# A decoder layer with 32 experts: the tensor engine's order per expert written out by hand

## The chip, the cores and the metric

The kernel runs on one core of a Trainium2 chip. The metric is device time in microseconds (us): the median of the runs shown, and for the profile the time of one profiled execution. PE is the tensor engine (TensorE), PEld its weight loads, DVE the vector engine, ACT the scalar engine, POOL GpSimd, and SP the engine whose queue issues nearly all DMA transfers.

## The reference

One layer of a decoder on 256 tokens of width 1024: a token mixer, a LayerNorm, a mixture of experts, a second LayerNorm. All is float32. The change is in the experts:

```python
logits = x @ router_w + router_b                  # 256 x 32
top_v, top_i = top_k(logits, 4);  gates = softmax(top_v)
# for each expert e, on the tokens that chose it:
h = x_e @ w1[e] + b1[e]                           # 1024 -> 2048
gate, up = split(h);  gate = min(gate, 7);  up = clip(up, -7, 7)
act = (up + 1) * (gate * sigmoid(1.702 * gate))
y_e = act @ w2[e] + b2[e]                         # 1024 -> 1024
out[token] += gate_weight * y_e
x = layer_norm(ALPHA * x + out)
```

## The kernel before

The mixer and the first LayerNorm take the first 270 us or so. Then come the experts, one after the other. Every expert's weights, 8 MB for the first product and 4 MB for the second, are read once from DRAM, in transfers of 1 MB (`load_w`, L76) that SP issues in order into a ring of buffers. A transfer waits until PE has read what lay in its buffer. In the loop, iteration e loads `w1` of expert e (8 transfers) and then `w2` of expert e-1 (4 transfers).

An expert has 64 slots. `slots` (L875, DVE) compares the tokens' ranks with the slot numbers and makes one-hot matrices `S` for two experts at once. `gather` (L882, PE) multiplies the tokens by them; `find` does this for experts e and e+1 in two halves of 16 instructions into two PSUM banks `u`, and `spread` (L982, ACT) copies the result to `xg`. `find` runs in even iterations.

What PE then does for one expert:

- `gemm1` (L1080): the first product, 64 instructions, into the banks `h0` and `h1`, with 64 rows of output in each half of the array. ACT (L1082) and DVE (L1083) copy the banks to `hs`.
- `act` (L1131): eight transposes of `hs` in two fours, each into a bank `u` that DVE evicts with the bias (L1132). Then the SwiGLU on DVE and ACT (L1135 to L1140), which gives `a`.
- `gemm2` (L1147): the second product of the expert before, 32 instructions into a bank `u`, copied to `ys` by ACT (L1149).
- `scatter_ops`: POOL (L1068) multiplies the slots by the gate weights, PE transposes the result (L1072), ACT copies it to `gT` (L1073).
- `scatter` (L1155): eight instructions that add `gT`ᵀ · `ys` to the four accumulation banks `acc`.

PSUM has eight banks: two `u` that take turns, `h0`, `h1`, four `acc`. The instructions of PE in the loop are issued on `nc.tensor` (through `te[0]`) up to expert 29: a planner sorts them, with those of the other engines, by its costs, and may put one expert's instructions between another's. An instruction issued through `PE` (L49) is kept in the order of the program. So the profile's order in the loop is the planner's: the second product is cut into four parts, with transposes, gathers and slot transposes between them.

After expert 13 (`MID`) the kernel tests whether an expert has more than 64 tokens (`overflow`, L1173); each engine branches over the body by itself. With the inputs of this case the body isn't run. The last two experts, 30 and 31, have orders of their own: the weights of expert 31 come in pieces of columns (L1261, L1290), and the second LayerNorm's statistics are taken as the columns are finished.

Of the kernel before, what the change touches and what calls it, by code (L numbers as in the profile page):

```python
# [20 lines left out]
T = 256  # L21
E = 32
# [13 lines left out]
MID = 13  # L36
# [16 lines left out]
def hybrid(ctx: ExitStack, tc: tile.TileContext, A, out, dbg=None):  # L53
    nc = tc.nc
# [38 lines left out]
    ident = consts.tile([128, 128], F32, name="ident")  # L93
# [51 lines left out]
    x = x1  # L145
# [785 lines left out]
    def u_tile():  # L931
        return ps.tile([128, 512], F32, name="u", bufs=2)
# [4 lines left out]
    def h_tile(c):  # L937
        return ps.tile([128, 512], F32, name=f"h{c}")
# [14 lines left out]
    def residuals():  # L953
        for t in range(2):
            for h in range(2):
                nc.tensor.matmul(acc[t][h], ident_a, x1[:, t, h * 512:(h + 1) * 512], start=False, stop=False,
                                 skip_group_check=True)

    xT = ext.rearrange("p (k c) -> p k c", k=8)
# [82 lines left out]
        nc.vector.tensor_copy(cnts[:, :E], p)  # L1042
        nc.vector.tensor_reduce(cnts[:, E:], p, axis=AX.X, op=OP.max)

    te = [nc.tensor]

    def find(e):

        slots(rk[:, :, e:e + 2], slice(0, 2))
        for h in range(2):  # L1050
            p = u_tile()
            for t in range(2):
                gather(p, t, HALF[h], 2, te[0])
            spread(e, h, p, nc.scalar.copy)

    def find_one(src, dst):
        slots(src, slice(0, 2))
# [2 lines left out]
            gather(p, t, range(8), 1)  # L1060
        nc.scalar.copy(dst, p.rearrange("p (k s) -> p k s", k=8))

    def scatter_ops(buf, gsrc, x):

        gT = ext[:, buf * T:(buf + 1) * T]
        SG = ext[:, 512:768].rearrange("p (t d s) -> p t d s", t=2, d=2)
        for t in range(2):
            nc.gpsimd.tensor_tensor(SG[:, t], S[:, t, x:x + 1].to_broadcast([128, 2, SLOTS]),  # L1068
                                    gsrc[:, t].unsqueeze(2).to_broadcast([128, 2, SLOTS]), op=OP.mult)
        p = u_tile()[:, :T]  # L1070
        for t in range(2):
            te[0].transpose(p[:, t * 128:(t + 1) * 128], SG[:, t].rearrange("p d s -> p (d s)"), ident)  # L1072
        nc.scalar.copy(gT, p)  # L1073
        return gT

    def gemm1(xg, w1):

        hp = [h_tile(c) for c in range(2)]
        for k, c, half in w1.order:
            te[0].matmul(hp[c][half * 64:(half + 1) * 64], xg[:, k],  # L1080
                             w1(k, half * 2 + c), start=(k == 0), stop=(k == 7), skip_group_check=True)
        nc.scalar.copy(hs[:, :512], hp[0])  # L1082
        nc.vector.tensor_copy(hs[:, 512:], hp[1])  # L1083
# [31 lines left out]
                return self.block('moe_w2', k, c)  # L1115
            return self.w[k // 2][:, k % 2, c * 512:(c + 1) * 512]

    def act(bias, a, g=None):

        bv = bias.rearrange("p (h j) -> p j h", h=2)  # L1120
        pieces = [slice(q * 4, (q + 1) * 4) for q in range(2)]
        js = slice(0, 8)
        if g is not None:
            js = slice(2 * g, 2 * g + 2)
            pieces = [js]
        for piece in pieces:
            n = piece.stop - piece.start
            p = u_tile()[:, :n * 128]
            for j in range(n):
                c = (piece.start + j) * 128  # L1130
                te[0].transpose(p[:, j * 128:(j + 1) * 128], hs[:, c:c + 128], ident)  # L1131
            nc.vector.tensor_tensor(hT[:, piece], p.rearrange("p (j h s) -> p j h s", j=n, h=2),  # L1132
                                    bv[:, piece, :].unsqueeze(3).to_broadcast([128, n, 2, SLOTS]), op=OP.add)
        gate, up = hT[:, js, 0, :], hT[:, js, 1, :]
        nc.vector.tensor_scalar(gate, gate, LIMIT, None, op0=OP.min)  # L1135
        sg = hs[:, js.start * 128:js.start * 128 + (js.stop - js.start) * 64].rearrange("p (j s) -> p j s", s=64)
        nc.scalar.activation(sg, gate, AF.Sigmoid, scale=1.702)
        nc.vector.tensor_scalar(up, up, LIMIT, -LIMIT, op0=OP.min, op1=OP.max)
        nc.vector.tensor_tensor(sg, sg, gate, op=OP.mult)
        nc.vector.scalar_tensor_tensor(a[:, js], up, 1.0, sg, op0=OP.add, op1=OP.mult)  # L1140
        return a

    def gemm2(a, w2):
        yp = u_tile()
        for k, c, half in w2.order:
            if c == 0:
                te[0].matmul(yp[half * 64:(half + 1) * 64, :], a[:, k], w2(k, half),  # L1147
                                 start=(k == 0), stop=(k == 7), skip_group_check=True)
        nc.scalar.copy(ys, yp)  # L1149

    def scatter(gT, first=False):
        for t in range(2):
            for half in range(2):
                r = slice(half * 64, (half + 1) * 64)
                te[0].matmul(acc[t][half], gT[r, t * 128:(t + 1) * 128], ys[r, :],  # L1155
                                 start=first, stop=False,
                                 skip_group_check=True)

    def gated_biases(b2r):
        p = u_tile()[:E, :T]  # L1160
        for t in range(2):
            te[0].transpose(p[:, t * 128:(t + 1) * 128], G[:, t, :], ident)
        GT = lp.tile([E, T], F32, name="GT")
        nc.vector.tensor_copy(GT, p)
        for t in range(2):
            for h in range(2):
                te[0].matmul(acc[t][h], GT[:, t * 128:(t + 1) * 128], b2r[:, h * 512:(h + 1) * 512],
                                 start=False, stop=False, skip_group_check=True)

    def overflow():  # L1170

        most = nc.values_load(cnts[0:1, E:E + 1], min_val=0, max_val=T)
        with tc.If(most > SLOTS):  # L1173
            with tc.For_i(0, E, 1) as ei:
                ce = nc.values_load(cnts[0:1, ds(ei, 1)], min_val=0, max_val=T)
                with tc.If(ce > SLOTS):
                    be = lp.tile([128, 16], F32, name="be")
                    nc.vector.tensor_copy(be.unsqueeze(2), b1T[:, :, ds(ei, 1)])
                    gev = lp.tile([128, 2, 1], F32, name="gev")
                    nc.vector.tensor_copy(gev, G[:, :, ds(ei, 1)])  # L1180
                    rke = lp.tile([128, 2, 1], F32, name="rke")
                    nc.vector.tensor_copy(rke, rk[:, :, ds(ei, 1)])
                    for _ in range(1, T // SLOTS):
                        nc.vector.tensor_scalar(rke, rke, float(SLOTS), None, op0=OP.subtract)
                        find_one(rke, xg[0])
                        gT = scatter_ops(0, gev, 0)
                        gemm1(xg[0], First(ei, True))
                        a = act(be, xg[1])
                        gemm2(a, Second(ei, True))
                        scatter(gT)  # L1190

    def norm_rows():

# [7 lines left out]
            nc.scalar.copy(gb2[:, q * 4:(q + 1) * 4], p.rearrange("p (j c) -> p j c", j=4))  # L1201
        return [gb2[:, i * 8:(i + 1) * 8].rearrange("p r c -> p (r c)") for i in range(2)]

    prev = None
    for e in range(E - 1):
        buf = e % 2
        if e:
            if buf == 0:
                find(e)
            gT = scatter_ops(buf, G[:, :, e:e + 1], buf)  # L1210
        if e == E - 3:
            g2, b2 = norm_rows()
        w1 = First(e).load()
        if 0 < e < E - 2:
            w2 = Second(e - 1).load()
        if e == SUMS:
            b2r = new_w()[:E, :D]
            nc.sync.dma_start(b2r, A['moe_b2'])
        if e == E - 2:
            te[0] = PE  # L1220
        gemm1(xg[e % 3], w1)
        if e == 0:
            p = u_tile()
            for c in range(4):
                PE.transpose(p[:, c * 128:(c + 1) * 128], b1r[:, c * 128:(c + 1) * 128], ident)
            nc.scalar.copy(b1T.rearrange("p (q c) e -> p c q e", q=4), p.rearrange("p (c q e) -> p c q e", c=4, q=4))
            with tc.issue_after(last_pe), tc.issue_after(last_act), tc.issue_after(last_dve):
                acc[1] = [acc_tile(1, h) for h in range(2)]
                gates_and_counts()
            gT = scatter_ops(0, G[:, :, 0:1], 0)  # L1230
            a = act(b1T[:, :, e], a_main)
        elif e < E - 3:
            gemm2(prev[0], w2)
            a = act(b1T[:, :, e], a_main)
            scatter(prev[1], e == 1)
            if e == SUMS:
                residuals()
                gated_biases(b2r)
        elif e == E - 3:

            a = act(b1T[:, :, e], xg[e % 3])
            gemm2(prev[0], w2)
            scatter(prev[1])
            gemm2(a, Second(e).load())
        else:
            a = act(b1T[:, :, e], a_main)
            scatter(prev[1])
            gTn = scatter_ops(1 - buf, G[:, :, E - 1:], 1)
            gemm2(a, Second(e).load())
        prev = (a, gT)  # L1250
        if e == MID:
            overflow()


# [98 lines left out]
```

## Time and profile before

| what | before |
|---|---|
| median of 3 runs | 1243.77 us (1243.24 to 1246.75) |
| the profiled execution, its own time | 1242.18 us |
| its span, first to last instruction | 1240.4 us |
| mean granted clock of TensorE in it | 0.994 |
| read from DRAM | 447.25 MB |

The span is what the rows below are measured in. The profiled execution takes 1.8 us more than its span, and its time is 1.6 us below the median of the runs shown.

### The profile page before, as it was taken

The numbers are of one execution on the slowest core, as the hardware profiler recorded it, in microseconds if no ns is written. First come the engines' busy times: TensorE is split into PE (matmuls) and PEld (weight loads), VectorE is DVE, ScalarE is ACT, GpSimd is POOL, SyncE is SP. The second block draws the span as 40 slices with busy tenths as digits, with TensorE's granted clock in tenths as the row PEclk, the third lists the DMA queues.
The fourth block names the chain that finished last, engine by engine and source line by source line (L and its number), as shares of the span: only waits on it lengthen the run. The fifth ranks groups of instructions, "written<-read, shape, count | busy, mean of one in ns | idle before, by whom it ended". The sixth has DMA issues, their size and how long they took to land. (4 is left out here: it accounts for less than half of the span.)

```text
span 1240.4 us, 15834 instructions
## 1 busy us (share of the span) xinstructions
PE 1155.3 (93%) x6554; PEld 594.1 (48%) x6555; DVE 362.3 (29%) x729; ACT 198.4 (16%) x483; POOL 66.4 (5%) x108
## 2 busy tenths in 40 slices
PE   8999999999999899999899799999999999999996
PEld 8899899883333233333333333333333333333344
DVE  7679777662111111101211011111111111111114
ACT  4115442422101010101010001000010101011111
POOL 1010002420000000000000000000000000000000
PEclk9999999999999999999999999999999999999998
DMA  8994367679999999999989999999999999999990
GB/s 239 335 317 143 103 204 314 254 294 393 417 417 417 418 417 408 416 417 417 417 361 417 416 417 417 417 417 417 417 417 417 417 418 417 417 417 413 387 284 34
DMA packets 127463, 449.39 MB, mean 362 GB/s; under 512 B 11205, under 2 KB 58235, under 8 KB 95643
## 3 DMA queue, kind: packets, MB, share of 16 engines
q1 hardware_dynamic: 127242, 448.06, 91.9%
q8 instruction: 54, 0.88, 0.3%
q10 hardware_dynamic: 144, 0.26, 0.1%
q14 instruction: 23, 0.18, 0.0%
HBM read 447.25 MB, written 1.05 MB: 361 GB/s over the span
## 5 line engine op out<-in xcount | busy, mean ns | idle before, releaser
L1080 PE MATMUL h<-w,t 128*64 128x512 f32 x1280 | 280.1, 594 | 0.0
L1147 PE MATMUL u<-w,t 128*64 128x512 f32 x928 | 223.2, 601 | 0.0
L1080 PEld LDWEIGHTS h<-w,t 128*64 128x64 f32 x1280 | 90.3, 137 | 180.2 <-issue 176.0
L1083 DVE COPY t<-h 128x512 f32<-128x512 f32 x31 | 21.4, 692 | 470.3 <-PE h L1080 437.7
L1080 PE MATMUL h<-w,rws 128*64 128x512 f32 x640 | 141.2, 600 | 0.0
L1147 PEld LDWEIGHTS u<-w,t 128*64 128x64 f32 x928 | 59.4, 136 | 94.9 <-issue 84.9
L88 PE MATMUL mm<-xh,ws 128*128 128x256 f32 x336 | 96.7, 288 | 0.0
L90 PE MATMUL mm<-xh,ws 128*128 128x256 f32 x336 | 95.0, 283 | 0.0
L89 PE MATMUL mm<-xl,ws 128*128 128x256 f32 x336 | 94.9, 283 | 0.0
L1080 PEld LDWEIGHTS h<-w,rws 128*64 128x64 f32 x640 | 45.4, 138 | 91.0 <-issue 88.3
L1132 DVE TENSOR_TENSOR t<-u,b1T 128x512 f32<-128x512 f32 (+1 forms) x66 | 44.6, 675 | 143.3 <-PE u L1131 122.8
L882 PE MATMUL u<-ext,x 128*128 128x128 f32 x480 | 70.2, 291 | 15.9 <-DVE t L1132 10.2
L882 PEld LDWEIGHTS u<-ext,x 128*128 128x128 f32 x480 | 59.3, 195 | 53.3 <-issue 39.6
L1082 ACT COPY t<-h 128x512 f32<-128x512 f32 x31 | 18.2, 586 | 391.4 <-PE h L1080 366.7
L1068 POOL TENSOR_TENSOR ext<-ext,G 128x128 f32<-128x128 f32 x64 | 26.3, 424 | 872.5 <-PE u L1072 806.9
L83 DVE TENSOR_TENSOR ws<-w,ws 128x1024 fp32r<-128x1024 f32 (+1 forms) x62 | 70.7, 1145 | 2.6 <-ACT ws L82 1.7
L1155 PE MATMUL acc<-t,ext 64*128 64x512 f32 x232 | 57.6, 615 | 14.4 <-ACT t L1149 14.4
L1131 PE MATMUL u<-ident,t 128*128 128x128 f32 x240 | 45.4, 293 | 22.2 <-DVE t L1132 22.0
L88 PEld LDWEIGHTS mm<-xh,ws 128*128 128x128 f32 x336 | 64.3, 191 | 0.6 <-issue 0.3
L90 PEld LDWEIGHTS mm<-xh,ws 128*128 128x128 f32 x336 | 64.2, 191 | 0.6 <-issue 0.4
L89 PEld LDWEIGHTS mm<-xl,ws 128*128 128x128 f32 x336 | 64.3, 191 | 0.0
L1131 PEld LDWEIGHTS u<-ident,t 128*128 128x128 f32 x240 | 26.0, 140 | 76.1 <-issue 46.2
(340 smaller groups left out, 1056.9 us busy)
## 6 DMA issues: line engine op xcount, KB each, us to landing
w<-in_moe_w_dram SPq DMA_DIRECT2D x375, 1024.0 KB
w<-in_w_in_dram SPq DMA_DIRECT2D x22, 1024.0 KB
w<-in_moe_w_dram SPq DMA_DIRECT2D x18, 512.0 KB
w<-in_w_up_dram SPq DMA_DIRECT2D x6, 1024.0 KB
w<-in_cmp_w_dram SPq DMA_DIRECT2D x4, 1024.0 KB
w<-in_w_o_dram SPq DMA_DIRECT2D x4, 1024.0 KB
w<-in_w_in_dram SPq DMA_DIRECT2D x6, 512.0 KB
x<-in_x_dram SPq DMA_DIRECT2D x4, 256.0 KB
```

Source lines behind the costliest of these rows:

```text
L83: return sub.tensor_tensor(lo, src, hi.bitcast(F32), op=OP.subtract).ins
L88: pe.matmul(p, ah, bh, start=first, stop=False, **kw)
L89: pe.matmul(p, ah, bl, start=False, stop=False, **kw)
L90: pe.matmul(p, al, bh, start=False, stop=last, **kw)
L882: i = pe.matmul(p[:, j * c:(j + 1) * c], x1[:, t, k * 128:(k + 1) * 128], S[:, t, :n].rearrange("p x s -> p (x s)"), start=(t == 0 and j = ...
L1068: nc.gpsimd.tensor_tensor(SG[:, t], S[:, t, x:x + 1].to_broadcast([128, 2, SLOTS]), gsrc[:, t].unsqueeze(2).to_broadcast([128, 2, SLOTS]), ...
L1080: te[0].matmul(hp[c][half * 64:(half + 1) * 64], xg[:, k], w1(k, half * 2 + c), start=(k == 0), stop=(k == 7), skip_group_check=True)
L1083: nc.vector.tensor_copy(hs[:, 512:], hp[1])
L1131: te[0].transpose(p[:, j * 128:(j + 1) * 128], hs[:, c:c + 128], ident)
L1132: nc.vector.tensor_tensor(hT[:, piece], p.rearrange("p (j h s) -> p j h s", j=n, h=2), bv[:, piece, :].unsqueeze(3).to_broadcast([128, n, ...
L1147: te[0].matmul(yp[half * 64:(half + 1) * 64, :], a[:, k], w2(k, half), start=(k == 0), stop=(k == 7), skip_group_check=True)
L1155: te[0].matmul(acc[t][half], gT[r, t * 128:(t + 1) * 128], ys[r, :], start=first, stop=False, skip_group_check=True)
```

## The change

PE's order in the loop is written out: every instruction of PE in it is issued through `PE` and stays in program order. `scatter` of an expert comes one iteration later, behind the next first product. The eight transposes of `act` follow in one go, the second four into `h0`. The gathers of `find` move to the odd iteration before, the first half into `h1` ahead of the second product, the second half behind it. The slot matrix's transposes go into `h1` (even) or `h0` (odd). `scatter_ops` is split: `weigh` (POOL) is issued before the first product, `turn_slots` (PE, ACT) where the order has it. Before the overflow test the outstanding `scatter` is done; the body of the test makes expert 14's tokens anew at its end. In the diff, the lines that only replace `te[0]` by `PE` are left out.

```diff
-    def find(e):
-
-        slots(rk[:, :, e:e + 2], slice(0, 2))
-        for h in range(2):
-            p = u_tile()
-            for t in range(2):
-                gather(p, t, HALF[h], 2, te[0])
-            spread(e, h, p, nc.scalar.copy)
+    def find(e, h, p):
+
+        for t in range(2):
+            gather(p, t, HALF[h], 2, PE)
+        spread(e, h, p, nc.scalar.copy)
...
-    def scatter_ops(buf, gsrc, x):
-
-        gT = ext[:, buf * T:(buf + 1) * T]
-        SG = ext[:, 512:768].rearrange("p (t d s) -> p t d s", t=2, d=2)
+    SG = ext[:, 512:768].rearrange("p (t d s) -> p t d s", t=2, d=2)
+
+    def weigh(gsrc, x):
+
         for t in range(2):
             nc.gpsimd.tensor_tensor(SG[:, t], S[:, t, x:x + 1].to_broadcast([128, 2, SLOTS]),
                                     gsrc[:, t].unsqueeze(2).to_broadcast([128, 2, SLOTS]), op=OP.mult)
-        p = u_tile()[:, :T]
-        for t in range(2):
-            te[0].transpose(p[:, t * 128:(t + 1) * 128], SG[:, t].rearrange("p d s -> p (d s)"), ident)
-        nc.scalar.copy(gT, p)
+
+    def turn_slots(buf, p):
+
+        gT = ext[:, buf * T:(buf + 1) * T]
+        for t in range(2):
+            PE.transpose(p[:, t * 128:(t + 1) * 128], SG[:, t].rearrange("p d s -> p (d s)"), ident)
+        nc.scalar.copy(gT, p[:, :T])
         return gT
...
-    def act(bias, a, g=None):
+    def act_steps(bias, a, g=None, banks=None):
...
-        for piece in pieces:
+        for i, piece in enumerate(pieces):
             n = piece.stop - piece.start
-            p = u_tile()[:, :n * 128]
+            p = (banks[i] if banks else u_tile())[:, :n * 128]
...
                                     bv[:, piece, :].unsqueeze(3).to_broadcast([128, n, 2, SLOTS]), op=OP.add)
+        yield
...
+    def act(*args, **kw):
+        for _ in act_steps(*args, **kw):
+            pass
+        return args[1]
...
+            slots(rk[:, :, MID + 1:MID + 3], slice(0, 2))
+            for h in range(2):
+                find(MID + 1, h, u_tile())
...
-    prev = None
+    prev = gT = late = None
     for e in range(E - 1):
-        buf = e % 2
-        if e:
-            if buf == 0:
-                find(e)
-            gT = scatter_ops(buf, G[:, :, e:e + 1], buf)
+        buf, odd = e % 2, e % 2 == 1
...
-        if e == E - 2:
-            te[0] = PE
+        if e:
+            weigh(gates(e), buf)
+            if odd:
+                slots(rk[:, :, e + 1:e + 3], slice(0, 2))
         gemm1(xg[e % 3], w1)
...
-        elif e < E - 3:
+        elif e < E - 2:
+            if late:
+                scatter(*late)
+                late = None
+            a = xg[e % 3] if e == E - 3 else a_main
+            steps = act_steps(b1T[:, :, e], a, banks=[u_tile(), h_tile(0)])
+            next(steps)
+            if odd:
+                find(e + 1, 0, h_tile(1))
+            else:
+                gT = turn_slots(buf, h_tile(1))
             gemm2(prev[0], w2)
-            a = act(b1T[:, :, e], a_main)
-            scatter(prev[1], e == 1)
+            for _ in steps:
+                pass
+            if odd:
+                gT = turn_slots(buf, h_tile(0))
+                find(e + 1, 1, u_tile())
+            late = prev[1], e == 1
             if e == SUMS:
+                scatter(*late)
+                late = None
                 residuals()
                 gated_biases(b2r)
-        elif e == E - 3:
-
-            a = act(b1T[:, :, e], xg[e % 3])
-            gemm2(prev[0], w2)
-            scatter(prev[1])
-            gemm2(a, Second(e).load())
+            if e == E - 3:
+
+                scatter(*late)
+                gemm2(a, Second(e).load())
         else:
             a = act(b1T[:, :, e], a_main)
             scatter(prev[1])
-            gTn = scatter_ops(1 - buf, G[:, :, E - 1:], 1)
+            gT = turn_slots(buf, u_tile())
+            weigh(gates(E - 1), 1)
+            gTn = turn_slots(1 - buf, u_tile())
             gemm2(a, Second(e).load())
         prev = (a, gT)
         if e == MID:
+            scatter(*late)
+            late = None
             overflow()
```

## Rows read from the trace of the kernel before

**Rows 1.** The page, parts 1 and 2: engines, and GB/s in 40 equal slices.
```profile
PE 1155.3 (93%) x6554; PEld 594.1 (48%) x6555; DVE 362.3 (29%) x729; ACT 198.4 (16%) x483; POOL 66.4 (5%) x108
...
GB/s 239 335 317 143 103 204 314 254 294 393 417 417 417 418 417 408 416 417 417 417 361 417 416 417 417 417 417 417 417 417 417 417 418 417 417 417 413 387 284 34
```
**Rows 2.** The page, parts 4 and 6: the chain by engine; weight transfers.
```profile
PE 41%; DVE 2%; ACT 1%; issue 0%; DVEq 0%; ACTq 0%
...
w<-in_moe_w_dram SPq DMA_DIRECT2D x375, 1024.0 KB
```
**Rows 3.** Windows of two experts: us, busy us, PE clock, DMA share, GB/s; first, last of seven.
```profile
693.15:751.75 58.60, 54.37 (x262) 20.48 (x264) 8.87 (x15) 5.45 (x13) 1.68 (x5) 1.00 1.02 417
...
1044.49:1103.04 58.55, 54.37 (x262) 20.51 (x264) 8.87 (x15) 5.45 (x13) 1.68 (x5) 1.00 1.02 417
```
**Rows 4.** Windows of the end, columns as in rows 3.
```profile
1160.00:1204.00 44.00, 42.27 (x222) 18.01 (x220) 4.13 (x7) 4.24 (x10) 0.76 (x2) 1.00 1.07 350
1204.00:1206.00 2.00, 2.00 (x22) 1.35 (x20) 0.00 (x0) 0.37 (x1) 0.00 (x0) 1.00 0.31 84
```
**Rows 5.** Timeline of PE, expert 31: last first-product piece, last 128 columns.
```profile
1214.75 1.95 PE L49 MATMUL h<-w,t 128*64 128x256 f32 x16
...
1228.25 1.09 PE L49 MATMUL u<-w,t 128*64 128x128 f32 x16
```
**Rows 6.** Timeline of PE, two experts: start, us, what, [idle before].
```profile
751.68 13.95 PE L1080 MATMUL h<-w,t 128*64 128x512 f32 x64
...
767.28 0.66 PE L1131 MATMUL u<-ident,t 128*128 128x128 f32 x4
768.72 0.33 PE L1131 MATMUL u<-ident,t 128*128 128x128 f32 x1 [0.78 <-DVE t L1132]
...
772.27 0.30 PE L1072 MATMUL u<-ident,ext 128*128 128x128 f32 x1 [0.88 <-DVE t L1132]
...
777.25 1.99 PE L1155 MATMUL acc<-t,ext 64*128 64x512 f32 x8 [0.68 <-ACT t L1149]
...
799.67 0.49 PE L882 MATMUL u<-ext,x 128*128 128x128 f32 x2 [0.78 <-DVE t L1132]
...
808.03 2.05 PE L882 MATMUL u<-ext,x 128*128 128x128 f32 x16
809.91 0.38 PE L1072 MATMUL u<-ident,ext 128*128 128x128 f32 x2
```
**Rows 7.** Timeline of PE, expert 29's second product of expert 28.
```profile
1151.30 7.09 PE L1147 MATMUL u<-w,t 128*64 128x512 f32 x32
```
**Rows 8.** SP's waits in 380 to 430 and in 880 to 930: us, times, longest.
```profile
SPq L76 <- PE h L1080: 28.6, 16, 6.3
...
SPq L76 <- DMA w<-in_moe_w_dram: 31.8, 17, 2.2
```
**Rows 9.** Line 1173, the overflow test: branches (ns, start us), who waited (us, times).
```profile
L1173 SPq COMPARE_BRANCH  x1: 50/50/50, 636.3 to 636.3; - x1
...
  DVE ext L875: 6.7, 1
```
**Rows 10.** Timeline of SP in 648 to 683.
```profile
648.67 34.24 SPq L76 DMA_DIRECT2D w<-in_moe_w_dram  x20
```
**Rows 11.** Windows of the middle, columns as in rows 3.
```profile
640.00:650.00 10.00, 8.34 (x41) 2.98 (x39) 2.78 (x5) 0.75 (x2) 0.00 (x0) 1.00 0.67 266
650.00:660.00 10.00, 9.31 (x43) 2.95 (x41) 1.44 (x3) 1.42 (x3) 0.00 (x0) 1.00 0.96 400
...
648.67:682.90 34.23, 30.71 (x138) 10.12 (x138) 6.95 (x12) 3.39 (x6) 0.00 (x0) 1.00 0.98 397
```
**Rows 12.** Windows with low PE shares, columns as in rows 3 (clock third from last).
```profile
240.00:248.00 8.00, 5.27 (x28) 4.12 (x28) 7.67 (x14) 4.55 (x8) 1.38 (x1) 1.00 0.50 193
...
680.00:690.00 10.00, 4.34 (x19) 3.08 (x20) 0.76 (x2) 0.23 (x1) 0.76 (x2) 0.87 1.01 419
690.00:700.00 10.00, 10.00 (x58) 5.25 (x59) 0.43 (x1) 1.57 (x5) 0.76 (x2) 0.96 1.01 408
```

More of the change, by code (lines that the diff above doesn't have):

```diff
@@ L955, in residuals @@
             for h in range(2):
-                nc.tensor.matmul(acc[t][h], ident_a, x1[:, t, h * 512:(h + 1) * 512], start=False, stop=False,
+                PE.matmul(acc[t][h], ident_a, x1[:, t, h * 512:(h + 1) * 512], start=False, stop=False,
                                  skip_group_check=True)
@@ L1079, in gemm1 @@
         for k, c, half in w1.order:
-            te[0].matmul(hp[c][half * 64:(half + 1) * 64], xg[:, k],
+            PE.matmul(hp[c][half * 64:(half + 1) * 64], xg[:, k],
                              w1(k, half * 2 + c), start=(k == 0), stop=(k == 7), skip_group_check=True)
@@ L1125, in act @@
             pieces = [js]
-        for piece in pieces:
+        for i, piece in enumerate(pieces):
             n = piece.stop - piece.start
-            p = u_tile()[:, :n * 128]
+            p = (banks[i] if banks else u_tile())[:, :n * 128]
             for j in range(n):
                 c = (piece.start + j) * 128
-                te[0].transpose(p[:, j * 128:(j + 1) * 128], hs[:, c:c + 128], ident)
+                PE.transpose(p[:, j * 128:(j + 1) * 128], hs[:, c:c + 128], ident)
             nc.vector.tensor_tensor(hT[:, piece], p.rearrange("p (j h s) -> p j h s", j=n, h=2),
                                     bv[:, piece, :].unsqueeze(3).to_broadcast([128, n, 2, SLOTS]), op=OP.add)
+        yield
         gate, up = hT[:, js, 0, :], hT[:, js, 1, :]
@@ L1140, in act @@
         nc.vector.scalar_tensor_tensor(a[:, js], up, 1.0, sg, op0=OP.add, op1=OP.mult)
-        return a
+    def act(*args, **kw):
+        for _ in act_steps(*args, **kw):
+            pass
+        return args[1]
     def gemm2(a, w2):
@@ L1146, in gemm2 @@
             if c == 0:
-                te[0].matmul(yp[half * 64:(half + 1) * 64, :], a[:, k], w2(k, half),
+                PE.matmul(yp[half * 64:(half + 1) * 64, :], a[:, k], w2(k, half),
                                  start=(k == 0), stop=(k == 7), skip_group_check=True)
@@ L1154, in scatter @@
                 r = slice(half * 64, (half + 1) * 64)
-                te[0].matmul(acc[t][half], gT[r, t * 128:(t + 1) * 128], ys[r, :],
+                PE.matmul(acc[t][half], gT[r, t * 128:(t + 1) * 128], ys[r, :],
                                  start=first, stop=False,
@@ L1161, in gated_biases @@
         for t in range(2):
-            te[0].transpose(p[:, t * 128:(t + 1) * 128], G[:, t, :], ident)
+            PE.transpose(p[:, t * 128:(t + 1) * 128], G[:, t, :], ident)
         GT = lp.tile([E, T], F32, name="GT")
@@ L1166, in gated_biases @@
             for h in range(2):
-                te[0].matmul(acc[t][h], GT[:, t * 128:(t + 1) * 128], b2r[:, h * 512:(h + 1) * 512],
+                PE.matmul(acc[t][h], GT[:, t * 128:(t + 1) * 128], b2r[:, h * 512:(h + 1) * 512],
                                  start=False, stop=False, skip_group_check=True)
@@ L1185, in overflow @@
                         find_one(rke, xg[0])
-                        gT = scatter_ops(0, gev, 0)
+                        weigh(gev, 0)
+                        gT = turn_slots(0, u_tile())
                         gemm1(xg[0], First(ei, True))
@@ L1202, in norm_rows, with gates @@
         return [gb2[:, i * 8:(i + 1) * 8].rearrange("p r c -> p (r c)") for i in range(2)]
-    prev = None
+    def gates(e):
+        return G[:, :, e:e + 1]
+    prev = gT = late = None
     for e in range(E - 1):
-        buf = e % 2
-        if e:
-            if buf == 0:
-                find(e)
-            gT = scatter_ops(buf, G[:, :, e:e + 1], buf)
+        buf, odd = e % 2, e % 2 == 1
         if e == E - 3:
@@ L1229, in hybrid @@
                 gates_and_counts()
-            gT = scatter_ops(0, G[:, :, 0:1], 0)
+            weigh(gates(0), 0)
+            gT = turn_slots(0, u_tile())
             a = act(b1T[:, :, e], a_main)
-        elif e < E - 3:
-            gemm2(prev[0], w2)
-            a = act(b1T[:, :, e], a_main)
-            scatter(prev[1], e == 1)
+        elif e < E - 2:
[9 more added lines that the diff above has]
+                gT = turn_slots(buf, h_tile(1))
+            gemm2(prev[0], w2)
+            for _ in steps:
[4 more added lines that the diff above has]
+            late = prev[1], e == 1
             if e == SUMS:
+                scatter(*late)
+                late = None
                 residuals()
                 gated_biases(b2r)
-        elif e == E - 3:
-            a = act(b1T[:, :, e], xg[e % 3])
-            gemm2(prev[0], w2)
-            scatter(prev[1])
-            gemm2(a, Second(e).load())
+            if e == E - 3:
+                scatter(*late)
+                gemm2(a, Second(e).load())
         else:
```

1 line of the change is left out of this document (removed).

## The prediction

> **What bounds the kernel now.** I read the page first. PE is busy 93% of the span and the GB/s line stands at 416 to 418 in nearly every slice from the eleventh on, with one dip to 361 (the 21st) and a fall in the last three [rows 1]. So two candidates are busy in the same stretch. The chain that ended last then names one: PE with small shares of DVE and ACT, no DMA [rows 2]. The windows, one for each two experts, say how the two stand: seven windows in a row take 58.54 to 58.60 us, PE busy 54.4 us of each, DMA at 417 GB/s in all [rows 3]. Two experts need 24 transfers of 1024 KB [rows 2], 25.17 MB; at 417 GB/s that is 60.35 us. PE uses 25.17 MB in 58.55 us, more than arrives. It can, because it draws on weights fetched ahead. PE sets the pace, and DMA, working all the time, is 1.8 us slower per two experts.
>
> So what PE can gain has a floor: the last weight. The windows of the end put it at about 1205 us, since DMA moves 84 GB/s in 1204 to 1206 and the stretch before runs at 350 GB/s with a DMA share over 1 [rows 4]. PE starts the product on the last 128 columns only at 1228.25, 23 us later [rows 5]. That lag is what a faster PE can remove. All the rest is DMA's, except a hole at the middle (below).
>
> **The change part by part.** *PE's order.* The timeline of two experts shows what an expert costs PE and where it stands still [rows 6]. First product: 13.95 us for 64 instructions. The four transposes of the second half, those of `find` and the one of the slot matrix each wait behind a DVE eviction: 0.78, 0.78 and 0.88 us idle. The scatter waits 0.68 us for ACT's copy of `ys`. The second product is cut in four by these. Where it is uncut (expert 29) its 32 instructions take 7.09 us [rows 7].
>
> The new order puts the scatter of the expert before behind the first product. Its 1.99 us cover the evictions of `hs` that the transposes need. Then come eight transposes, then 16 gathers (odd e) or two slot transposes (even e), then the uncut second product, and for odd e two slot transposes and 16 gathers. The 16 gathers need ACT's two copies before the next first product gets to k=4, some 7 us into it, so they aren't waited for. For two experts PE has, by [rows 6, 7]: 2 x 13.95 + 2 x 7.09 + 2 x 1.99 + 4 x 0.66 (transposes in fours) + 2 x 2.05 (gathers in sixteens) + 2 x 0.38 (slot transposes) = 53.6 us. The groups overlap by under 0.1 us at each of 14 seams, so 52.6 to 53.6; I take 53. PE's pace falls from 58.55 to 53 us, 5.5 us per two experts, and 14 such pairs would give 77 us.
>
> *What the banks cost.* The transposes, gathers and slot matrices now use the two banks of the first product between its runs, so the next first product waits for their readers. The latest is ACT's copy of the slot matrix in h0 (odd e). It starts after ACT's copy of `ys`, while PE has 2.05 us of gathers ahead of it. I cost it at nothing. If the copies ran one behind the other after the gathers, it would be under 1 us per two experts, which the 5.5 us still cover.
>
> *SP and the weights.* The order of the weight transfers is unchanged. Early, SP waits for PE alone to free buffers; later it waits mostly for its own earlier transfers [rows 8], so there the number in flight is the limit. A faster PE brings that state forward and, with it, a DMA that never waits for a buffer. It doesn't bring more bytes per us: the late slices have the same 417 as the early ones [rows 1].
>
> *The middle.* After expert 13 comes the test for overflow. SP meets its branch at 636.3 [rows 9] and issues nothing until 648.67 [rows 10], while the transfers in flight run out: 266 GB/s in 640 to 650 [rows 11]. That is (417 - 266) / 417 x 10 = 3.6 us of DMA lost, with the ten us after it (400 GB/s) 4.0 us. From 648.67 to 682.90 SP issues 20 transfers (21.0 MB) while 34.23 us at 397 GB/s bring 13.6 MB, so 7 can be in flight at once [rows 10, 11]. Seven last 17.6 us, more than SP's 12.4. By then the new PE is some 6 pairs x 5.5 = 33 us ahead, which frees 13 more buffers, so the queue should be at its limit at the branch and the hole closes: 4 us. Bounds: 0 (it stays as it is) to 4. I take 4, since the state needed is that of [rows 8], second row.
>
> *PE's own branch.* DVE sat 6.7 us on PE's branch before the slots of expert 14 [rows 9], and PE's gathers wait for these. The new kernel gathers expert 14 before the test, so PE resumes with weights at once. PE is by then ahead of or level with DMA, so this gives nothing at the end.
>
> *Last experts.* In expert 30 both slot matrices are now made after the first product, the second behind a POOL multiply that waits for the first transposes. That is about 1.2 us of PE stall (two POOL instructions near 0.4 us and the hand-overs, an estimate; the bound below is nothing). DMA covers it: four transfers of the second weights still arrive, 10 us.
>
> **The sum.** The last weight arrives at 1205 - 4 = 1201. The last expert's second weights are 4.19 MB (three transfers of 1024 KB, two of 512), 12.0 us at 350 GB/s, so its last first-product piece is there at 1189. From the start of that piece's product to the start of the last 128 columns PE needed 1228.25 - 1214.75 = 13.5 us [rows 5], so this starts at 1202.5, 25.7 us earlier than now. Each piece before takes PE 1.95 us and the DMA 3.0 (1024 KB), so PE keeps up. What follows 1228.25 is unchanged. The span goes from 1240.4 to 1214.7, the profiled execution from 1242.18 to 1216.5. The median of the runs shown lies 1.6 us above that execution, so the time is 1218.
>
> While PE waits for each weight, its clock may fall. In 240 to 248 PE was busy 5.27 of 8 us and was granted full clock; in 680 to 690, when it stood still for over 5 us, the mean was 0.87 and then 0.96, that is part of the time at the lower of the two levels, 1.2 instead of 2.4 GHz [rows 12]. The new waits are short (1.75 us of work, an eighth of 13.95, per 2.5 us transfer), nearer the first row, so I keep full clock. The Trainium skill's page "TensorE: Matmul & The Clock Gate", section "HAM oscillation — how this bites in real kernels", tells of a kernel that waited for DMA between its k-tiles and lost its full clock at every one. This kernel will wait in just that place. The page's waits were longer than its work; here they are shorter. By that rule the time would be that of the two clock rivals below, 1229 or 1277.
>
> **Rivals.** *The hole stays* (10%): 4 us less gain, 1222; for it speaks only that SP's branch is untouched. *The clock falls in the last expert* (9%): at half speed a piece takes 3.9 us against 3.0, eight pieces are 7 us late, and part of the 13.5 us behind them doubles, up to 1229. For it: the tail has PE's lowest share of work. Against: [rows 12], first row. *PE alone sets the end* (2%), as the chain [rows 2] has it: 77 us less, 1165. DMA would have to move the same bytes some 9% faster, about 455 GB/s, which no slice shows.
>
> *Slower than before* (4%): the clock drops and stays low from the middle on. One half-speed us loses 0.5 us. Slack is 9 pairs x 7.35 us (60.35 - 53) plus the 26 us won, 92 us, so it decides the case from some 185 us at the lower level; 250 us would give about 1277. Against it: a PE at half speed is busy without a break, and in [rows 12] the clock was coming back in the next stretch. *No change* (4%): PE gains less than about 0.5 us per pair, for instance because the order written out is nearly the one that now runs with a new stall (a bank, an ACT copy) in place of each old one. Saving at least 26 us takes only 1.9 us per pair of the 5.5, so a third is enough for the full forecast.
>
> **Numbers.** The forecast has 71%. About 0.3% is what this kernel's measurement can tell from no change. Faster 0.92, same 0.04, slower 0.04. The range runs from 1210 (1 to 2% fewer lost DMA us in the tail, hole closed, no PE lag at the end) to 1229 (clock in the tail) and leaves out the cases of no change, slower and PE alone.
>
> **What would show it.** Right: windows of two experts near 53 us before the middle and near 60.4 behind it, PEld or PE waiting for DMA of `w` in the second half, SP waiting for its own transfers, no dip in the GB/s line at the middle, the last weights near 1201 and the last product within 2 us of them. Wrong: pairs still near 58 us with PE waits for ACT or DVE at the `h` banks; a granted clock below 1 in the second half; the dip still there.

## The result, and the profile after

| what | before | after |
|---|---|---|
| median | 1243.74 us (1243.24 to 1246.75), 4 runs | 1223.89 us (1222.58 to 1225.73), 4 runs |
| ratio to before | | 0.984, interval 0.982 to 0.986 |
| the profiled execution | 1242.18 us | 1225.73 us |
| its span | 1240.4 us | 1223.7 us |

The change takes 19.9 us off, 1.6%; the forecast was 1218. The page of the kernel after, parts 1 (PE alone), 2 and 4:

```profile
PE 1142.7 (93%) x6554; PEld 589.1 (48%) x6555; DVE 358.4 (29%) x729; ACT 197.8 (16%) x483; POOL 68.3 (6%) x108
...
PEclk9999999999999999999999999999999999999999
...
GB/s 240 325 313 146 128 207 266 285 265 362 417 417 417 418 416 413 405 417 418 417 417 357 416 417 417 417 417 417 418 417 417 416 418 417 417 418 416 417 361 192
...
DMA 30%; PE 15%; DVE 1%; SPq 0%; issue 0%; POOL 0%
```

PE is as busy as in [rows 1], 93%, but the chain that ended last now runs through DMA, which [rows 2] didn't name at all. The GB/s line still has a dip (357, the 22nd slice), and its last slice holds 192 instead of 34: the weights now last almost to the end. Two experts before the middle, two behind it, the middle and the end as windows (columns as in [rows 3]):

```profile
427.56:479.25 51.69, 51.69 (x261) 20.67 (x260) 8.60 (x15) 5.43 (x12) 1.77 (x4) 1.00 1.02 418
...
895.10:955.30 60.20, 53.19 (x250) 18.35 (x250) 8.54 (x15) 5.21 (x12) 1.10 (x3) 1.00 1.02 417
...
640.00:650.00 10.00, 10.00 (x59) 5.06 (x58) 2.26 (x5) 2.02 (x5) 0.00 (x0) 1.00 0.92 374
650.00:660.00 10.00, 8.30 (x40) 3.33 (x40) 0.00 (x0) 0.65 (x2) 0.76 (x2) 1.00 0.72 275
...
1204.00:1209.00 5.00, 4.96 (x37) 3.29 (x34) 0.93 (x4) 0.74 (x2) 0.00 (x0) 1.00 0.76 207
1209.00:1212.00 3.00, 3.00 (x31) 2.11 (x31) 1.72 (x8) 0.27 (x1) 0.00 (x0) 1.00 0.00 1
```

PE's own pace is 51.69 us for two experts without a gap, where [rows 3] had 58.55. Behind the middle two experts take 60.20 us at 417 GB/s: the DMA's pace, at PE's full clock. The last weight is there at about 1209 (1 GB/s behind it), where [rows 4] put it at 1205. The timeline of PE, late in the kernel and in expert 31:

```profile
905.86 1.94 PE L49 MATMUL h<-w,t 128*64 128x512 f32 x8 [0.45 <-DMA w<-in_moe_w_dram]
908.35 1.94 PE L49 MATMUL h<-w,t 128*64 128x512 f32 x8 [0.55 <-DMA w<-in_moe_w_dram]
...
912.71 1.99 PE L49 MATMUL acc<-t,ext 64*128 64x512 f32 x8
914.62 0.66 PE L49 MATMUL u<-ident,t 128*128 128x128 f32 x4
915.12 0.60 PE L49 MATMUL h<-ident,t 128*128 128x128 f32 x4
915.55 0.38 PE L49 MATMUL h<-ident,ext 128*128 128x128 f32 x2
915.87 7.11 PE L49 MATMUL u<-w,t 128*64 128x512 f32 x32
...
1211.53 1.09 PE L49 MATMUL u<-w,t 128*64 128x128 f32 x16
```

The four waits of [rows 6] for DVE and ACT are gone, and the second product runs uncut in 7.1 us. In their place the first product waits some 0.55 us for most of its weight transfers. The last 128 columns start at 1211.53, 2.4 us behind the last weight; in [rows 5] they lagged 23 us.

### The profile page after: what moved, and what is told of

Its sections match the earlier page's. It is cut to its first block, busy times and chain, and to the rows that moved or that the text cites. A ratio compares the mean times of both kernels' runs of the same rounds, so it can differ in the third digit from the quotient of the medians.

```text
span 1223.7 us, 15821 instructions
## 1 busy us (share of the span) xinstructions
PE 1142.7 (93%) x6554; PEld 589.1 (48%) x6555; DVE 358.4 (29%) x729; ACT 197.8 (16%) x483; POOL 68.3 (6%) x108
## 5 line engine op out<-in xcount | busy, mean ns | idle before, releaser
L49 PE MATMUL h<-w,t 128*64 128x512 f32 (+1 forms) x1472 | 324.7, 580 | 39.9 <-DMA w<-in_moe_w_dram 38.8
L49 PE MATMUL u<-w,t 128*64 128x512 f32 (+2 forms) x1040 | 222.2, 577 | 1.8 <-DMA w<-in_moe_w_dram 1.7
L49 PEld LDWEIGHTS h<-w,t 128*64 128x64 f32 x1472 | 99.3, 137 | 256.0 <-issue 155.3
L1081 DVE COPY t<-h 128x512 f32<-128x512 f32 x31 | 21.4, 692 | 534.4 <-PE h L49 534.4
L49 PEld LDWEIGHTS u<-w,t 128*64 128x64 f32 x1040 | 70.9, 137 | 130.1 <-issue 114.8
L49 PE MATMUL acc<-t,ext 64*128 64x512 f32 (+2 forms) x268 | 66.4, 596 | 0.9 <-ACT t L1153 0.7
L1140 DVE SCALAR_TENSOR_TENSOR t<-t 128x512 f32<-128x512 f32 (+1 forms) x34 | 22.0, 648 | 144.9 <-PE u L49 144.7
L1153 ACT COPY t<-u 128x512 f32<-128x512 f32 x31 | 18.2, 586 | 174.0 <-PE u L49 174.0
L1131 DVE TENSOR_TENSOR t<-u,b1T 128x512 f32<-128x512 f32 (+1 forms) x37 | 24.4, 661 | 71.9 <-PE u L49 71.9
L82 DVE CAST ws<-w 128x1024 fp32r<-128x1024 f32 (+1 forms) x57 | 38.2, 678 | 23.7 <-PE mm L90 16.9
L49 PEld LDWEIGHTS acc<-t,ext 64*128 64x128 f32 (+1 forms) x268 | 24.4, 186 | 39.7 <-issue 28.0
```

The lines of the kernel that those rows point to most:

```text
L49: return lambda *a, **k: self.tc.keep_in_program_order(f(*a, **k))
L82: copy(hi, src)
```

## The experiments

Times are medians; the kernel before, run beside them on the same chip, had 1244.2 to 1244.6 us. Four were run together on one chip: half the weights (in both kernels), program order alone, the test left out. Four on another: three more tests, the test moved, three-fold transposes, and the kernel after once more. Then three on one chip: five-fold transposes, the scatter, POOL's queue.

**Half of the first-product weights.** Each transfer serves two `k`; the rest of the program is the same, but an expert has 8 transfers instead of 12, and the output isn't the reference's. The edit, in the kernel after and in the one before:

```diff
-            self.w = [load_w(w1v[self.e][:, k:k + 1, :], 1, 2048) for k in range(8)]
+            four = [load_w(w1v[self.e][:, k:k + 1, :], 1, 2048) for k in range(0, 8, 2)]
+            self.w = [four[k // 2] for k in range(8)]
```

> The changed kernel, but of the first weights of experts 0 to 30 only every second of the eight 1024 KB tiles is loaded and used twice (that part of the product is of other numbers): 8 instead of 12 transfers per expert, PE's work the same. Theory (after the middle DMA alone sets the pace, PE alone would do two experts in about 52 us): 16 transfers take 40 us, so PE's pace rules throughout, two experts take 51 to 53 us everywhere and the time is 1140 to 1165. Rival (PE has become slower in its second half for a reason of its own, clock or banks): two experts stay near 60 us behind the middle and the time stays near 1224.

> The same cut of the transfers in the kernel before. Theory (there PE's pace of 58.55 us per two experts rules from end to end, and DMA takes no part): 1238 to 1246, two experts still 58.5 us. Rival (before, too, PE's pace was held by the transfers, through buffers or memory traffic): clearly below 1235.

After: 1152.33 us (ratio 0.925, 0.923 to 0.928). With a third of the expert weights left out, DMA moves 313 GB/s in a window behind the middle, and PE is busy for all 120 us of it:

```profile
900.00:1020.00 120.00, 120.00 (x614) 49.25 (x615) 20.20 (x36) 13.53 (x31) 4.55 (x10) 1.00 0.84 313
```

So DMA was what held the new kernel. Before: 1172.51 us (0.941, 0.939 to 0.943), which the expectation missed by over 60 us. The reason is in PE's timeline and windows of that kernel, second half:

```profile
730.93 7.04 PE L1148 MATMUL u<-w,t 128*64 128x512 f32 x32
737.90 0.66 PE L1132 MATMUL u<-ident,t 128*128 128x128 f32 x4
...
717.15:770.40 53.25, 53.11 (x262) 20.87 (x261) 8.95 (x15) 5.55 (x13) 2.22 (x4) 1.00 0.83 320
```

The edit touches no instruction of PE, and yet their order is another: the planner's order depends on the transfers. With fewer of them it left the second product all but whole, and two experts took 53.25 us instead of 58.55. So the run is no clean control: transfers and order changed together. The next experiment changes the order alone.

**Program order alone.** The kernel before with one line changed; the scatter, the banks and the gathers stay as they were.

```diff
-    te = [nc.tensor]
+    te = [PE]
```

> The kernel before with one line changed: PE's instructions in the loop are kept in the order of its program, in which the second product is uncut and the scatter follows the transposes; none of the three parts of the change (late scatter, transposes in one go, shared banks). Theory (what counts is that PE saves some 2 us of 58.55 per two experts, then the last weight sets the end): I work out 53 to 56 us per two experts, with a wait of 1 to 2 us for the slots in even iterations, and the time is 1221 to 1228, as with the whole change. Rival (the whole new order is needed): 1235 to 1250.

1225.97 us (0.984, 0.982 to 0.986): the whole gain of the change, from one line, with every transfer in place. So the planner's order was what held the kernel before. Its windows of two experts, before the middle and about two behind it, and its PE timeline:

```profile
432.70:485.10 52.40, 52.09 (x261) 20.68 (x260) 8.95 (x15) 5.46 (x13) 2.22 (x4) 1.00 1.02 417
890.00:950.00 60.00, 53.41 (x258) 19.58 (x258) 8.95 (x15) 5.54 (x12) 2.22 (x4) 1.00 1.02 417
...
454.26 0.66 PE L49 MATMUL u<-ident,t 128*128 128x128 f32 x4 [0.15 <-ACT t L1149]
```

52.40 us, 0.7 more than the order written out, with waits of 0.15 us; the 1 to 2 us expected for the slots don't appear. Both are under the DMA's 60.35, so the difference is worth nothing here.

**The scatter where it was.** The kernel after, with each expert's scatter right behind its second product.

```diff
-            late = prev[1], e == 1
+            scatter(prev[1], e == 1)
```

> The changed kernel with the scatter of an expert right behind its second product again, not one expert later; all else as written out. Theory: PE now waits for ACT's copy of the second product (about 0.7 us) and, behind the first product, for the copies of hs that the scatter covered (about 1 us), so early pairs go from 51.7 to 53 to 56 us, still below the DMA's 60.35: the time stays at 1222 to 1228 us. Rival: the later scatter is the part of the change that carries the gain; then pairs are near 58 us and the time 1235 us or more.

1225.36 us (0.984, 0.980 to 0.988), as the theory had it. PE's timeline of one expert in it:

```profile
447.24 0.66 PE L49 MATMUL h<-ident,t 128*128 128x128 f32 x4 [0.21 <-DVE t L1081]
...
455.81 1.99 PE L49 MATMUL acc<-t,ext 64*128 64x512 f32 x8 [0.68 <-ACT t L1153]
```

The later scatter saves these two waits, 0.9 us an expert, and the time doesn't show it.

**How much slack PE has.** Each of the eight transposes of experts 1 to 29 is done three times, or five times.

```diff
-                PE.transpose(p[:, j * 128:(j + 1) * 128], hs[:, c:c + 128], ident)
+                for _ in range(3 if banks else 1):
+                    PE.transpose(p[:, j * 128:(j + 1) * 128], hs[:, c:c + 128], ident)
```

> The changed kernel with each of the eight transposes of an expert done three times (same result): 2.3 us of PE work more per expert, 4.6 per pair, 56.3 instead of 51.7 us. Theory (PE has about 8.5 us of slack per pair against DMA's 60.2 and some lead to build up): the time stays at 1222 to 1228; pairs of about 56 us until the lead is used, later than in the changed kernel, then 60.2. Rival (what PE saves is what the kernel saves, 20 us for 14 pairs, so a third of it or more comes back): 1240 or more, as 14 x 4.6 us are 64.

> The changed kernel with each of the eight transposes of experts 1 to 29 done five times (the repeats write the same values). Three times made the first pairs 55.2 us long instead of 51.7, 3.5 us for two repeats, so five times should make them about 58.7 us, the pace of the kernel before (58.55). Theory: what counts is PE's time for an expert and nothing else of the new order. Then the gain is gone: 1238 to 1249 us, no waits of PE for weights in the second half, and a lag of some 20 us or more from the last weight to the last product. Rival: part of the gain comes from elsewhere (the transfers' order, the loads after the test, the last two experts); then the time stays at 1224 to 1236 with the same 58.7 us pairs.

Three times: 1225.88 us (0.985, 0.982 to 0.987), no change, though a pair before the middle takes 55.2 us (56.3 was expected). Its first products start at:

```profile
435.87 13.95 PE L49 MATMUL h<-w,t 128*64 128x512 f32 x64
...
491.06 9.23 PE L49 MATMUL h<-w,rws 128*64 128x512 f32 x42
```

Five times: 1249.05 us (1.003, 1.001 to 1.005), and the gain is gone. Windows of 120 us before and behind the middle, and the last 128 columns:

```profile
320.00:440.00 120.00, 120.00 (x662) 56.23 (x660) 17.56 (x30) 10.86 (x24) 3.54 (x8) 1.00 1.02 417
...
900.00:1020.00 120.00, 120.00 (x662) 56.23 (x660) 17.56 (x30) 10.86 (x24) 3.54 (x8) 1.00 1.02 417
...
1235.90 1.09 PE L49 MATMUL u<-w,t 128*64 128x128 f32 x16
```

PE is busy for all of both, at the 417 GB/s that [rows 3] has too. The last weight lands at 1213.8, so the last columns lag it by 22 us, as in the kernel before. PE's first products start 58.68 us apart, two experts later (898.35 and 957.03). So all else of the new order, with PE's time for two experts put back to its old size, gives the old time. Of the 4.4 us above the kernel before on the same chip, 14 pairs at 0.13 us more would make 1.8, and 2.0 are the later start that the last experiment finds (294.9 in this kernel against 292.9); the rest isn't accounted for.

**The overflow test.** Four edits: the test left out (the inputs of this case don't need it), three more tests of the same kind behind experts 17, 21 and 25, the test moved to the end ahead of expert 31's products (with expert 31's loads put ahead of it in the program), and the kernel after once more.

```diff
-            overflow()
...
-        if e == MID:
+        if e in (MID, 17, 21, 25):
...
+    overflow()
     banks = [h_tile(c) for c in range(2)]
```

> The changed kernel without the test for overflow after expert 13 (with these inputs its body is not run). Theory (at the test SP waits for each of its own transfers in flight to land before it issues the next, so DMA stands still about 4.4 us however many are in flight): no dip in the middle, the time is 4 to 5 us under the changed kernel's 1223.9, 1219 to 1220. Rival (the hole costs nothing at the end, since PE has stock): 1223 to 1225.

> The changed kernel once more, as the yardstick for the kernels beside it: 1222 to 1226.

> The changed kernel with the test behind experts 13, 17, 21 and 25 instead of behind 13 alone (its body is not run). Theory: each test empties the transfers in flight and costs DMA about 4.4 us, so three more cost 13 us: 1235 to 1239, with four dips in the DMA rate. Rival (a test costs the end little, 1 us): 1226 to 1228.

> The changed kernel with the overflow test moved from behind expert 13 to the place where SP has issued the last weight of all (before expert 31 is computed); with these inputs its body is not run in either place. Theory (at the test SP lets all its transfers land before it issues another, and as DMA sets the end that hole of 4.4 us is paid in full): no dip in the middle, 3 to 5 us under the changed kernel run beside it, 1219 to 1221, with PE's branch hidden behind the last weights. Rival (the hole is not paid at the end, as the 1.1 us of the kernel without the test may say): within 1.5 us of the changed kernel.

Left out: 1222.83 us (0.982, 0.981 to 0.984), which misses the theory's 1219 to 1220 and lies just under the rival's 1223 to 1225. Again: 1226.09 (0.985, 0.983 to 0.988). Three more: 1235.71 (0.993, 0.990 to 0.995), as expected, 9.6 us above the unchanged kernel on the same chip, 3.2 for each test. Moved: 1225.32 (0.984, 0.982 to 0.986), 0.8 us under that kernel where 3 to 5 were expected, so no gain. Windows of the middle without the test, of the second and third test, and of the middle and the end with the test moved:

```profile
640.00:650.00 10.00, 10.00 (x59) 4.95 (x59) 1.99 (x4) 2.11 (x6) 1.02 (x2) 1.00 1.02 418
650.00:660.00 10.00, 10.00 (x48) 3.33 (x48) 0.00 (x0) 0.56 (x2) 0.00 (x0) 1.00 1.02 424
```
```profile
765.00:790.00 25.00, 23.04 (x124) 10.63 (x122) 3.44 (x6) 2.67 (x7) 0.76 (x2) 1.00 0.89 357
890.00:915.00 25.00, 23.03 (x124) 10.61 (x122) 3.44 (x6) 2.67 (x7) 0.76 (x2) 1.00 0.89 357
```
```profile
640.00:650.00 10.00, 10.00 (x56) 4.53 (x54) 1.39 (x2) 2.34 (x7) 1.01 (x2) 1.00 1.02 418
650.00:660.00 10.00, 9.67 (x44) 2.78 (x40) 0.00 (x0) 0.00 (x0) 0.00 (x0) 1.00 1.01 420
1170.00:1180.00 10.00, 6.73 (x40) 3.04 (x38) 0.00 (x0) 0.58 (x1) 0.00 (x0) 1.00 0.62 212
```

Every test makes its own hole: (417 - 357) / 417 x 25 = 3.6 us of DMA at each of the added ones. Moving the test only moves the hole: against the 350 GB/s of that stage in [rows 4], (350 - 212) / 350 x 10 = 3.9 us are lost in 1170 to 1180. Most of expert 31's loads were scheduled behind the test all the same: SP issues five of its 21 ahead of the branch at 1168.5.

**Another queue in the hole.** The first-product weights of expert 14 are asked for ahead of the test, on POOL's queue.

```diff
-    def load_w(src, k, c):
+    def load_w(src, k, c, q=nc.sync):
...
-        i = nc.sync.dma_start(v, src)
+        i = q.dma_start(v, src)
...
-            self.w = [load_w(w1v[self.e][:, k:k + 1, :], 1, 2048) for k in range(8)]
+            self.w = [load_w(w1v[self.e][:, k:k + 1, :], 1, 2048,
+                             nc.gpsimd if self.e == MID + 1 and k < 8 else nc.sync) for k in range(8)]
...
-        w1 = First(e).load()
+        w1 = w1 if e == MID + 1 else First(e).load()
...
+            w1 = First(e + 1).load()
             overflow()
```

> The changed kernel with the first-product weights of expert 14 asked for ahead of the overflow test and issued by POOL, on its own queue; as scheduled, five of the eight are issued before the test and three behind it. Theory: the hole at the test is there because SP waits for all of its own transfers at the branch and only then issues again; transfers of another queue that are still in flight then fill the hole: 640 to 660 shows less than 2 us of DMA lost (4.4 now), the last weight comes at about 1206 instead of 1209, and the time is 1219 to 1224 us. Rival: the branch costs the same whatever queue is busy, because the engines wait for POOL's transfers too (or POOL's issue waits for SP's transfers first): the hole stays at 4 us or grows, 1224 to 1232 us.

1226.32 us (0.984, 0.980 to 0.988): no gain, and the hole stays. That is the rival's outcome; its reason isn't shown. The windows of the middle, then POOL's and PE's timelines:

```profile
630.00:640.00 10.00, 7.36 (x16) 1.54 (x16) 0.00 (x0) 0.00 (x0) 1.05 (x2) 0.50 1.01 422
640.00:650.00 10.00, 5.31 (x16) 1.25 (x16) 0.00 (x0) 0.00 (x0) 0.54 (x1) 0.84 1.01 421
650.00:660.00 10.00, 8.47 (x35) 3.11 (x36) 1.16 (x2) 0.58 (x1) 0.00 (x0) 0.83 1.01 410
660.00:670.00 10.00, 10.00 (x60) 5.07 (x59) 2.97 (x6) 2.02 (x5) 0.00 (x0) 1.00 0.57 211
```
```profile
627.08 0.53 POOL L76 DMA_DIRECT2D w<-in_moe_w_dram  x1 [4.43 <-DMA w<-in_moe_w_dram]
632.04 0.53 POOL L76 DMA_DIRECT2D w<-in_moe_w_dram  x1 [4.43 <-DMA w<-in_moe_w_dram]
```
```profile
620.37 1.94 PE L49 MATMUL h<-w,t 128*64 128x512 f32 x8 [2.80 <-DMA w<-in_moe_w_dram]
625.25 2.96 PE L49 MATMUL h<-w,t 128*64 128x512 f32 x8 [2.94 <-DMA w<-in_moe_w_dram]
630.21 3.68 PE L49 MATMUL h<-w,t 128*64 128x512 f32 x8 [2.01 <-DMA w<-in_moe_w_dram]
```

POOL's transfers took their share at once: while both queues were busy, POOL issued and SP landed one about every 5 us, and PE, waiting for SP's, fell behind. SP met its branch at 644.0, 10 us later than in the kernel after, and its last waits end at 657.9, 660.5, 663.0 and 665.5, 2.5 us apart again, so that POOL's transfers had landed by then. The hole moves to 660 to 670 and is no smaller. Whether transfers of another queue, still in flight when SP's last one lands, would fill it stays untried.

**The kernel before once more**, for a difference ahead of the experts. Its windows of 240 to 260 and those of the kernel after, in this order, from the first profiles:

```profile
240.00:260.00 20.00, 17.27 (x81) 14.05 (x81) 13.21 (x19) 8.94 (x12) 1.38 (x1) 1.00 0.67 253
```
```profile
240.00:260.00 20.00, 17.27 (x80) 14.13 (x79) 13.39 (x18) 9.01 (x13) 2.23 (x1) 0.91 0.60 219
```

> The kernel before, unchanged. In its profile the first expert's copies come at 292.9 us; in the profiles of the changed kernel and of its variants at 294.4 to 298.4, with 7 GB/s less in 200 to 300 us (314 instead of 321) and a stretch of TensorE at the lower clock level near 245 us that the kernel before doesn't show. Theory: this is scatter of single executions from before the experts, not the change: here too the first copies come at 294 to 298, the granted clock dips near 245, the GB/s of 200 to 300 lie at 313 to 318, and as PE's order then sets the end, the span is 1241 to 1244 us. Rival: the change moves work ahead of the experts: then the copies come at 293 again with 320 GB/s or more and a span of 1240 to 1241.

1244.49 us (1.000, 0.998 to 1.003). The theory fell: its first copies come at 293.0 us, 321 GB/s in 200 to 300, clock 1.00 in 240 to 250, as in the first profile of before. The lines of the first `h` copy to `hs`, before (L1083) and after (L1081):

```profile
L1083 DVE COPY t<-h x31: 691/692/693, 292.9 to 1187.3; 128x512 f32<-128x512 f32 x31
```
```profile
L1081 DVE COPY t<-h x31: 691/692/692, 295.1 to 1165.3; 128x512 f32<-128x512 f32 x31
```

So the kernel after reaches the first expert 2.2 us later, though each engine has the same instructions in the same order up to there. It isn't of the new order alone: the kernel before with program order, and that with half the weights, start later too (295.7 and 294.8). Set side by side, PE's instructions show where the time goes: 0.86 us are lost in the first 27 us, then nothing until 245, then 1.33 us within 2 us. PE's timeline there, before and after:

```profile
245.37 0.50 PE L88 MATMUL mm<-ys,mgh 128*128 128x512 f32 x1 [2.01 <-DVE gate L538]
245.70 0.39 PE L89 MATMUL mm<-ys,mgh 128*128 128x512 f32 x1
```
```profile
246.22 0.80 PE L88 MATMUL mm<-ys,mgh 128*128 128x512 f32 x1 [2.02 <-DVE gate L538]
246.81 0.63 PE L89 MATMUL mm<-ys,mgh 128*128 128x512 f32 x1
```

Behind the same wait for DVE seven instructions take 0.53 to 0.80 us instead of 0.39 to 0.50: the granted clock is 0.50 in 246 to 249, the lower of its two levels, where the kernel before has 1.00. That makes the 1.33 us. Why the clock falls there in one kernel and not in the other, and where the first 0.86 us come from, stays open.

## Why the prediction was right, and where it missed

**What bounds the kernel.** Right: PE set the end before, and DMA behind it had 23 us to give back. Half the weights, three-fold and five-fold transposes show it from both sides: less DMA makes the new kernel faster at once, and more PE work costs nothing at 55.2 us a pair and the whole gain at 58.7.

**PE's order.** Right in kind. The pair took 51.69 us, the forecast 53 (52.6 to 53.6). 14 seams at 0.1 us would already reach 52.2, and the seams among the transposes overlap by 0.16 and 0.17 us; the second four transposes took 0.60 us and not 0.66, 16 gathers 1.95 and not 2.05. The difference was worth nothing behind the middle, where DMA sets the pace. The banks cost nothing: no wait for an `h` or `u` bank stands in PE's timeline of two experts. PE's own branch went as forecast too: PE waits 1.70 us for it, where it waited 5.37 for the slots before. What brings the gain is program order, in which the second product stays uncut; the scatter one expert later adds slack alone. The prediction didn't part these two.

**SP and the weights.** Right: 60.20 us for two experts behind the middle (forecast near 60.4), and SP waits for its own transfers. In the late window of [rows 8] that wait now takes 33.0 us of 50, against 31.8 before; in the early one it already takes 26.3, where PE alone had been the cause.

**The middle: the step that failed.** The text said: "Seven last 17.6 us, more than SP's 12.4", so the hole closes, 4 us. It took 12.4 us for a time that SP needs by itself. The rows of SP at the branch, after (the line's instructions, then SP's waits in 625 to 665):

```profile
L1177 SPq EVENT_SEMAPHORE  x9: 17/17/17, 638.8 to 652.0; - x9
...
L1177 SPq COMPARE_BRANCH  x1: 50/50/50, 633.6 to 633.6; - x1
```
```profile
SPq L1177 <- SPq L1177: 18.2, 7, 5.2
```

SP's time at the branch grew with the queue: 18.2 us in seven waits, where the same row of before has 11.8 us in four. The nine semaphore instructions are the cause. Read one by one, they end at 638.8 and 638.9, then 639.4, 642.0, 644.5, 647.0, 649.5 and 651.9 to 652.0. The six waits that end from 639.4 to 651.9 lie 2.5 us apart, one 1 MB transfer at 417 GB/s each, and in the trace eight of the nine instructions wait for the eight semaphores that SP's own loads signal, one each. The kernel before has it too: its last three waits end at 643.5, 646.0 and 648.4, so the trace at hand could have told it. So SP waits until all that it has issued has landed, and only then issues again, from 652.1. However many are in flight, they are used up by then. The hole is what comes behind: the way of the first new transfers, 1.0 us lost in 640 to 650 and 3.4 in 650 to 660, 4.4 in all against 4.0 before. The three more tests cost 3.2 us of time each. Without the test the last weight comes at 1205.6, and the span is 3.5 us shorter than in the first profile of the kernel after and 2.6 shorter than in its second (1222.7). In the medians it is 1.1 and 3.3 us: the kernel after itself had 1223.89 and 1226.09. So the outcome is the rival *the hole stays*, 1222, to which I gave 10%, and the text's own sign of being wrong, the dip still there, came true; what spoke for that rival, SP's branch left untouched, was the point.

**The end.** Forecast for the last weight 1201, measured 1209.1. By the numbers above 4.4 us of this are the hole and 2.2 the later start of the experts; 1.5 remain. From the last weight to the end of the span it took 14.5 us, forecast 13.7. Together 8.9 us of span. As the profiled execution of after lies 1.8 us above its median, where I had put that of before 1.6 below, 5.9 us remain between 1218 and 1223.89. That the miss isn't 9 us is luck: 3.4 us of it are hidden by where two single executions fell among their runs.

**The clock.** The forecast held: full clock in the second half, PE busy 53.19 of 60.20 us, with waits of 0.55 us behind 1.94 us of work. In the run with POOL's queue the clock fell: behind waits of 2.80 and 2.94 us, longer than the 1.94 us of work, the same eight instructions took 2.96 and 3.68 us, with a granted clock of 0.50 in 630 to 640, the lower of the two levels. The Trainium skill's page "TensorE: Matmul & The Clock Gate", section "HAM oscillation — how this bites in real kernels", tells of a kernel whose waits for DMA were longer than the work between them and which lost the full clock at every one. The run with POOL's queue is that case, and there the trace agrees; the kernel after is not. So the prediction was right to go by the length of the waits, at 0.55 us. The length doesn't tell everything: behind the same wait of 2.0 us near 245 the clock was full in the kernel before and had fallen in the kernel after.

**Last experts.** Right: in expert 30 PE waits twice for POOL, 0.69 and 0.48 us; the estimate was 1.2 in all, hidden as said.

## What to carry to other kernels

When two resources are busy all through, find the lag between the last byte and the last product: it is what a faster engine can win, and half of the saving (55.2 us for two experts, between 51.7 and 58.55) won all of it here. Before writing an order out, try plain program order: here one line gave the whole gain, and the rest bought slack. A pause that a queue makes should not be priced against its fill until it is known whether it waits for that fill; look at its instructions one by one.

## What the hardware showed that was not expected

A branch on a value known only at run time, not taken, cost 3.2 us of time for each added one and 3.6 to 4.4 us of DMA wherever it stood among the loads, as SP waits at its end for all the transfers that it issued. And the stretch ahead of the experts, with the same instructions in the same order, had TensorE's clock at 0.91 in 240 to 260 in the kernel after and at 1.00 before, with equal busy time (17.27 of 20 us) and 34 GB/s less. All twelve profiles of kernels with an edited loop had a granted clock of 0.73 to 0.87 in 240 to 250 and the later start (294.4 to 298.4 us), and both profiles of the kernel before had neither; what in the program does it stays open.
